# The adaLN modulation of a hybrid trunk: streaming its matrix past silu(c) in the kernel's opening

## The chip, the cores and the metric

The kernel runs on one core of one Trainium2 chip. The metric is the device time of one execution in microseconds; of several runs the median is given. The trace is of one profiled execution, with times from the start of its span.

## The reference, cut to what matters

One layer of a diffusion backbone (DEPTH is 1, so only the RG-LRU mixer and the SwiGLU run), on 2048 latent tokens and 256 context tokens of width 1024, all in float32:

```python
act_lat, act_ctx = silu(c), silu(c_ctx)
mx = split(act_lat @ mod_w + mod_b, 6)        # shift, scale, gate of both sub-layers
mc = split(act_ctx @ mod_w + mod_b, 6)
hx = rms_norm(x, g_mix) * (1 + mx[1]) + mx[0]
hc = rms_norm(ctx, g_mix) * (1 + mc[1]) + mc[0]
x = x + mx[2] * rglru_mixer(hc, hx)
x = x + mx[5] * swiglu(rms_norm(x, g_ffn) * (1 + mx[4]) + mx[3])
```

The opening needs the first two of the six parts, shift and scale, for the latents and for the context: two vectors of 1024 times a 1024 x 2048 matrix of 8 MB. The other four are needed much later, for the latents alone.

## The kernel before

The kernel works on transposed activations: 128 channels on the partitions, tokens along the free axis. `D` = 1024 channels are `KD` = 8 tiles; `C` = 512 tokens are one half of a super-tile of `S` = 1024. Large products run as three fp32r products each (`mm3`, lines 106 to 108: high x high, high x low, low x high); `parts` (lines 83 and 84) makes such a pair of an operand, a cast on ScalarE and the remainder on VectorE.

`sweep1` runs the RG-LRU over two super-tiles; `sweep2` does the output product, the second norm and the feed-forward. The change is in `begin`, the opening of `sweep1`. There the order on TensorE, ScalarE and VectorE is the order of the program text (`manual_schedule`); only the DMA queue of SyncE is ordered by a planner. A buffer of a tag is handed on when its last user is done. The tags that matter: `raw` (4 buffers of 1024 columns), `op` (6), `hx` (8), and `p2`, four PSUM pairs, one for each product in flight.

What `begin` does, in order:

1. Constants; silu of c and c_ctx (`self.sc`, 128 x 8 x 2) on ScalarE; `silu_row` spreads silu(c) over the partitions with two products of a diagonal (lines 138 and 142) and copies it (L212). `decay` computes the recurrence's constants on VectorE, with one Exp on ScalarE.
2. The modulation in four quarters q of 512 outputs (0 and 1: shift and scale of the first four channel tiles; 2 and 3: of the last four). `mod_load` fetches a quarter as two halves of 1 MB into `op` buffers. `mod_half` (L228) makes each 128 x 128 piece of the matrix the stationary operand and multiplies the two silu columns with it, so the result comes out with channels on the partitions. `mod_apply` adds the bias and makes `A` (scale) and `B` (shift).
3. `column_stats` (L284, L287, L288) sums squares of the context and of the first 512 latents over channel tiles: a square on ScalarE, a sum on VectorE. Small products (L602) finish the sums, `rstd_of` (L123 to L130) takes the inverse root in sixteen small VectorE steps, and `spread` with `bc_sbuf` (L148) makes rows of it that are equal on all partitions.
4. `apply`, for one channel tile: VectorE scales (L305), ScalarE adds the shift and casts (L306, the high part), VectorE takes the remainder (L307). Tiles 0 to 3 of the first half run while TensorE is in quarters 2 and 3; tiles 4 to 7 follow `mod_apply` of these, each with one `token_stats` (L275, squares of 128 tokens of the second half).
5. The first half of the first rec product (`project`, 8 tiles x 3 products of 512 columns), of the gate product, then the spread row of the second half (L340, L341), the context (`apply_context`, four pairs of tiles, the row's spread standing behind the first), its rec product, `apply` of the second half, and the second halves of rec and gate. Behind it `blocks` runs the other nineteen channel blocks.

The turn between the super-tiles (L740, L750, L751) already mixes `apply` of two tiles: the scale of tile k + 4 stands behind the remainder of tile k.

## Time and profile before

| | us |
|---|---|
| median of 3 runs | 2342.04 |
| lowest, highest | 2341.98, 2343.08 |
| the profiled execution | 2343.92 |
| its span | 2342.2 |
| TensorE busy | 2253.5 (96%) |
| VectorE busy | 1489.7 (64%) |
| ScalarE busy | 1156.4 (49%) |
| mean granted TensorE clock | 0.975 |

Engines are PE (TensorE's products), PEld (its weight loads, which overlap), DVE (VectorE), ACT (ScalarE), POOL and SP (the DMA queue). A busy PE is not a PE at its peak: products overlap and their ends are modelled, so the distance from one start to the next tells more than the length.

### The profile page before, as it was taken

The page shows a single profiled execution, that of the slowest core. Times are in us where ns is not written, and L with a number is a line of the kernel's source. Part 1 is how long each engine was busy: PE and PEld are TensorE (multiplying, and loading weights), DVE is VectorE, ACT ScalarE, POOL GpSimd, SP SyncE. Part 2 cuts the span into 40 slices and gives each one's busy share as a digit, 9 for nine tenths or more (in the row PEclk, how much of TensorE's full clock was granted, in tenths as well). Part 3 has the DMA queues.
Part 4 walks back from the last instruction along what each step waited for, and adds up shares of the span by engine and source line. Part 5 has one row for each costly group of instructions (what it writes and reads, how often), then busy time and mean ns, then how long its engine had stood idle before and what let it go on. Part 6 is the DMA issues. An engine that isn't in the chain of part 4 may idle for free.

```text
span 2342.2 us, 25844 instructions
## 1 busy us (share of the span) xinstructions
PE 2253.5 (96%) x9852; PEld 1852.4 (79%) x9852; DVE 1489.7 (64%) x1912; ACT 1156.4 (49%) x1399; POOL 0.7 (0%) x6
## 2 busy tenths in 40 slices
PE   8899999899999958999999999999999999999999
PEld 8578887688887846878787888778888888888887
DVE  4567888678887577676666546864555555545443
ACT  2357775687776335565646334443333333333332
POOL 0000000000000000000000000000000000000000
PEclk9799999999999978999999999999999999999999
DMA  7135555221114733434343666776422222236664
GB/s 280 41 140 207 204 178 207 85 73 63 63 63 154 250 127 112 150 127 164 126 163 121 204 227 225 242 263 232 162 81 81 81 81 81 87 129 224 227 215 143
DMA packets 126556, 356.23 MB, mean 152 GB/s; under 512 B 15072, under 2 KB 15072, under 8 KB 125408
## 3 DMA queue, kind: packets, MB, share of 16 engines
q1 hardware_dynamic: 126432, 354.58, 44.5%
q8 instruction: 77, 1.26, 0.2%
q14 instruction: 47, 0.39, 0.0%
HBM read 283.22 MB, written 71.30 MB: 151 GB/s over the span
## 4 chain that ended last, share of the span: by engine, by line
PE 68%; ACT 7%; DVE 3%; issue 2%; DMA 1%; SPq 0%; DVEq 0%; ACTq 0%
PE ps_dn L107 6%; PE ps_dn L108 6%; PE ps_dn L106 6%; PE ps_be L106 6%; PE ps_be L107 6%; PE ps_be L108 6%; PE ps_ep L108 3%; PE ps_ep L107 3%; PE ps_ep L106 3%; PE ps_wo L106 3%; PE ps_wo L107 3%; PE ps_wo L108 3%; ACT L77 2%; PE ps_rec L108 2%; PE ps_rec L107 2%
## 5 line engine op out<-in xcount | busy, mean ns | idle before, releaser
L107 PE MATMUL ps_dn<-op_xd,op_wd 128*128 128x512 f32 x704 | 275.2, 391 | 1.9 <-DVE op_xd L84 1.8
L108 PE MATMUL ps_dn<-op_xd,op_wd 128*128 128x512 f32 x704 | 274.7, 390 | 0.0
L106 PE MATMUL ps_dn<-op_xd,op_wd 128*128 128x512 f32 x704 | 270.4, 391 | 1.6 <-ACT op_xd L83 1.6
L84 DVE TENSOR_TENSOR op_wd<-raw_wd,op_wd 128x1024 fp32r<-128x1024 f32 x88 | 107.7, 1223 | 200.2 <-ACT op_wd L83 200.1
L83 ACT CAST op_wd<-raw_wd 128x1024 fp32r<-128x1024 f32 x88 | 92.7, 1053 | 270.1 <-PE ps_dn L108 221.1
L950 DVE TENSOR_TENSOR s<-ps_ep,s 128x512 f32<-128x512 f32 x88 | 60.6, 688 | 154.1 <-ACT s L975 104.9
L107 PEld LDWEIGHTS ps_dn<-op_xd,op_wd 128*128 128x128 f32 x704 | 132.6, 188 | 30.8 <-DVE op_xd L84 3.2
L106 PEld LDWEIGHTS ps_dn<-op_xd,op_wd 128*128 128x128 f32 x704 | 132.1, 188 | 30.2 <-ACT op_xd L83 2.4
L108 PEld LDWEIGHTS ps_dn<-op_xd,op_wd 128*128 128x128 f32 x704 | 132.7, 189 | 27.6
L106 PE MATMUL ps_be<-T,op_b 128*128 128x512 f32 x352 | 139.5, 396 | 9.5 <-ACT s L975 9.5
L77 ACT ACT_TABLE_LOAD x113 | 145.0, 1283 | 2.7 <-PEq L1109 0.7
L106 PE MATMUL ps_ep<-T,op_s 128*128 128x512 f32 x352 | 138.3, 394 | 8.3 <-ACT T L890 8.3
L108 PE MATMUL ps_be<-T,op_b 128*128 128x512 f32 x352 | 138.4, 393 | 0.0
L107 PE MATMUL ps_be<-T,op_b 128*128 128x512 f32 x352 | 138.2, 393 | 0.0
L387 DVE SCALAR_TENSOR_TENSOR u<-ps_rec,c_conv_w,u 128x1024 f32<-128x1024 f32 x60 | 77.1, 1285 | 95.2 <-ACT u L384 93.6
L107 PE MATMUL ps_ep<-T,op_s 128*128 128x512 f32 x352 | 137.4, 390 | 0.0
L108 PE MATMUL ps_ep<-T,op_s 128*128 128x512 f32 x352 | 137.4, 390 | 0.0
L108 PE MATMUL ps_gate<-hx,op_g 128*128 128x512 f32 x320 | 127.0, 397 | 5.5 <-DVE op_g L84 5.5
L106 PE MATMUL ps_rec<-hx,op_r 128*128 128x512 f32 x320 | 129.6, 405 | 2.1 <-ACT hx L306 2.1
L107 PE MATMUL ps_rec<-hx,op_r 128*128 128x512 f32 x320 | 129.4, 404 | 0.6 <-DVE hx L307 0.6
L975 ACT COPY s<-ps_be 128x512 f32<-128x512 f32 x44 | 25.6, 583 | 207.8 <-PE ps_be L108 207.8
L108 PE MATMUL ps_rec<-hx,op_r 128*128 128x512 f32 x320 | 127.7, 399 | 0.0
(256 smaller groups left out, 5380.4 us busy)
## 6 DMA issues: line engine op xcount, KB each, us to landing
raw_wd<-in_down SPq DMA_DIRECT2D x88, 512.0 KB, 3.6
raw_xd<-d_act SPq DMA_DIRECT2D x88, 512.0 KB, 4.6
raw_ga<-in_gu SPq DMA_DIRECT2D x44, 512.0 KB, 3.9
raw_gb<-in_gu SPq DMA_DIRECT2D x44, 512.0 KB, 4.3
d_act<-s SPq DMA_DIRECT2D x88, 256.0 KB, 3.5
raw_xo<-d_rg SPq DMA_DIRECT2D x40, 512.0 KB, 4.2
raw_mod<-in_mod_t SPq DMA_DIRECT2D x32, 512.0 KB, 5.4
x<-in_x_t SPq DMA_DIRECT2D x48, 256.0 KB, 5.7
```

Source lines behind the costliest of these rows:

```text
L77: return self.table(self.nc.scalar.activation(out, in_, func, bias=bias, scale=scale))
L83: nc.scalar.copy(t[:, 0, :], raw)
L84: nc.vector.tensor_tensor(out=t[:, 1, :], in0=raw, in1=t[:, 0, :].bitcast(F32), op=ALU.subtract)
L106: ins = mm(ps, w[0], x[0], start=first, stop=False, skip_group_check=shared)
L107: mm(ps, w[0], x[1], start=False, stop=False, skip_group_check=shared)
L108: mm(ps, w[1], x[0], start=False, stop=last, skip_group_check=shared)
L387: v.scalar_tensor_tensor(out=part, in0=ps, scalar=cw[:, i : i + 1], in1=part, op0=ALU.mult, op1=ALU.add)
L950: v.tensor_tensor(out=t, in0=ps, in1=t, op=ALU.add)
L975: nc.scalar.copy(s3, be)
```

## The change

Six parts. (1) `mod_quarter` takes the place of `mod_half` and `mod_bank`: the silu columns become the stationary operand, four columns wide, and the matrix streams past, 512 columns at a time. Of its eight k the first four run in plain float32 (`mod_z`: the two silu columns and two zero columns); the other four are split into high and low parts by `parts`, against `mod_st`, whose four columns are the high parts of silu and the remainders. The result is four rows; ScalarE copies them to a `raw` tile and small products with `sel` turn them back into columns, adding high and low rows. (2) The quarters are loaded into `hx` buffers, where the tiles made of the input go later. (3) The first rec weight is loaded into a `raw` buffer at the start, and all four quarters before the second x halves. (4) `apply` takes a list and puts the scale of the next tile behind the cast of this one. (5) The order in `begin`: quarter 0, context sums, quarter 1, `decay`, latent sums, the weight's split, quarter 2, rows, tiles 0 to 3, quarter 3, the four `token_stats` together, tiles 4 to 7. (6) `apply_context` takes all eight context tiles in one list, behind the gate product and the spread row.

```diff
--- before.py
+++ after.py
...
             row = self.spread(self.sc[:, 4 * q : 4 * q + 4, 0], f"silu{q}")
             self.nc.vector.tensor_copy(self.sc_row[:, q * C : (q + 1) * C], row)
+    def mod_operands(self):
+        nc = self.nc
+        z = self.cp.tile([P, KD, 4], F32, name="mod_z")
+        nc.vector.memset(z, 0.0)
+        nc.vector.tensor_copy(z[:, :, 0:2], self.sc)
+        st = self.cp.tile([P, KD, 4], F32R, name="mod_st")
+        nc.vector.tensor_copy(st, z)
+        nc.vector.tensor_tensor(out=st[:, :, 2:4], in0=self.sc, in1=st[:, :, 0:2].bitcast(F32), op=ALU.subtract)
+        sel = self.cp.tile([P, 2], F32, name="sel")
+        nc.vector.tensor_tensor(out=sel, in0=self.ident[:, 0:2], in1=self.ident[:, 2:4], op=ALU.add)
+        self.mod_z, self.mod_st, self.sel = z, st, sel
     def mod_load(self, q):
         ts = []
         for half in range(2):
-            t = self.wp.tile([P, KD // 2, C], F32, tag="op", name=f"modf{q}_{half}", bufs=OPS)
+            t = self.hp.tile([P, KD // 2, C], F32, tag="hx", name=f"modf{q}_{half}", bufs=KD)
             self.nc.sync.dma_start(t, self.io["mod_f"][q, half])
             ts.append(t)
         return ts
-    def mod_half(self, ps, t, half):
-        for kk in range(KD // 2):
-            k = half * (KD // 2) + kk
-            for i in range(4):
-                self.nc.tensor.matmul(ps[:, i, :], t[:, kk, i * P : (i + 1) * P], self.sc[:, k, :],
-                                      start=(k == i == 0), stop=(k == KD - 1 and i == 3), skip_group_check=True)
-    def mod_bank(self, q):
-        return self.bank(f"ps_mod{q}")[:, :8].rearrange("p (i s) -> p i s", s=2)
+    def mod_split(self, ts, q):
+        return [self.parts(ts[1][:, 2 * j : 2 * j + 2, :].rearrange("p a c -> p (a c)"), f"modf{q}_{j}")
+                for j in range(2)]
+    def mod_quarter(self, q, ts, hl):
+        nc = self.nc
+        ps = self.bank(f"ps_mod{q}")[:4]
+        for k in range(4):
+            nc.tensor.matmul(ps, self.mod_z[:, k, :], ts[0][:, k, :], start=(k == 0), stop=False)
+        for k in range(4, KD):
+            for w in range(2):
+                x = hl[(k - 4) // 2][:, w, (k % 2) * C : (k % 2 + 1) * C]
+                nc.tensor.matmul(ps, self.mod_st[:, k, :], x, start=False, stop=(k == KD - 1 and w == 1))
+        rows = self.wp.tile([P, S], F32, tag="raw", name=f"mod_rows{q}", bufs=RAWS)[:4, :C]
+        nc.scalar.copy(rows, ps)
+        pc = self.bank(f"ps_modc{q}")[:, :8].rearrange("p (i s) -> p i s", s=2)
+        for i in range(4):
+            nc.tensor.matmul(pc[:, i, :], rows[:, i * P : (i + 1) * P], self.sel[:4],
+                             start=(i == 0), stop=(i == 3), skip_group_check=True)
+        return pc
     def mod_apply(self, q, pc):
...
             v.tensor_tensor(out=x, in0=x, in1=wide(self.A), op=ALU.mult)
             v.tensor_tensor(out=x, in0=x, in1=wide(self.B), op=ALU.add)
-    def apply(self, x, bc, a, b, h, l):
+    def apply(self, items):
         v = self.nc.vector
-        v.scalar_tensor_tensor(out=x, in0=x, scalar=a, in1=bc, op0=ALU.mult, op1=ALU.mult)
-        self.nc.scalar.activation(h, x, AF.Identity, bias=b, scale=1.0)
-        v.scalar_tensor_tensor(out=l, in0=x, scalar=b, in1=h.bitcast(F32), op0=ALU.add, op1=ALU.subtract)
-    def apply_context(self, j, xc, bc):
-        nc = self.nc
-        t = self.hp.tile([P, 2, 2, TX], F32R, tag="hc", name=f"hc{j}", bufs=4)
-        for i in range(2):
-            k = 2 * j + i
-            self.apply(xc[:, k % 4, :TC], bc, self.A[:, k, 1:2], self.B[:, k, 1:2], t[:, i, 0, :TC], t[:, i, 1, :TC])
-        x = xc[:, 2 * j % 4 : 2 * j % 4 + 2, TC:]
-        nc.scalar.copy(t[:, :, 0, TC:], x)
-        nc.vector.tensor_tensor(out=t[:, :, 1, TC:], in0=x, in1=t[:, :, 0, TC:].bitcast(F32), op=ALU.subtract)
-        self.hc += [(t[:, i, 0, :], t[:, i, 1, :]) for i in range(2)]
+        def scale(x, bc, a, b, h, l):
+            v.scalar_tensor_tensor(out=x, in0=x, scalar=a, in1=bc, op0=ALU.mult, op1=ALU.mult)
+        scale(*items[0])
+        for i, (x, bc, a, b, h, l) in enumerate(items):
+            self.nc.scalar.activation(h, x, AF.Identity, bias=b, scale=1.0)
+            if i + 1 < len(items):
+                scale(*items[i + 1])
+            v.scalar_tensor_tensor(out=l, in0=x, scalar=b, in1=h.bitcast(F32), op0=ALU.add, op1=ALU.subtract)
+    def apply_context(self, xc, bc):
+        nc = self.nc
+        ts = [self.hp.tile([P, 2, 2, TX], F32R, tag="hc", name=f"hc{j}", bufs=4) for j in range(KD // 2)]
+        self.context_extra(xc, bc[:, 3 * P - 2 : 3 * P])
+        for j, t in enumerate(ts):
+            nc.scalar.copy(t[:, :, 0, TC:], xc[j // 2][:, 2 * j % 4 : 2 * j % 4 + 2, TC:])
+        self.apply([(xc[k // 4][:, k % 4, :TC], bc[:, :TC], self.A[:, k, 1:2], self.B[:, k, 1:2],
+                     ts[k // 2][:, k % 2, 0, :TC], ts[k // 2][:, k % 2, 1, :TC]) for k in range(KD)])
+        for j, t in enumerate(ts):
+            x = xc[j // 2][:, 2 * j % 4 : 2 * j % 4 + 2, TC:]
+            nc.vector.tensor_tensor(out=t[:, :, 1, TC:], in0=x, in1=t[:, :, 0, TC:].bitcast(F32), op=ALU.subtract)
+        self.hc = [(ts[k // 2][:, k % 2, 0, :], ts[k // 2][:, k % 2, 1, :]) for k in range(KD)]
     def hx_tiles(self, s):
         ts = [self.hp.tile([P, 2, S], F32R, tag="hx", name=f"hx{s}_{k}", bufs=KD) for k in range(KD)]
...
         self.A = self.cp.tile([P, KD, 2], F32, name="A_mix")
         self.B = self.cp.tile([P, KD, 2], F32, name="B_mix")
+        raw_r = self.raw(io["w_rec"][0], "r0")
+        mod[2] = self.mod_load(2)
+        mod[3] = self.mod_load(3)
+        self.constants_rest()
+        a, b = (lambda k: self.A[:, k, 0:1]), (lambda k: self.B[:, k, 0:1])
+        first, second = slice(0, C), slice(C, S)
+        self.mod_operands()
         self.silu_row()
+        pm, hl = {}, {}
+        hl[0] = self.mod_split(mod[0], 0)
+        pm[0] = self.mod_quarter(0, mod[0], hl[0])
+        acc = [self.column_stats([xc[k // 4][:, k % 4, :] for k in range(KD)], TX, "c")]
+        hl[1] = self.mod_split(mod[1], 1)
+        pm[1] = self.mod_quarter(1, mod[1], hl[1])
         self.decay()
-        pm = {q: self.mod_bank(q) for q in range(2)}
-        for q in range(2):
-            for half in range(2):
-                self.mod_half(pm[q], mod[q][half], half)
-        mod[2] = self.mod_load(2)
-        acc = [self.column_stats([xc[k // 4][:, k % 4, :] for k in range(KD)], TX, "c"),
-               self.column_stats([x0[k][:, :C] for k in range(KD)], C, "x")]
-        mod[3] = self.mod_load(3)
         for q in range(2):
             self.mod_apply(q, pm[q])
+        acc.append(self.column_stats([x0[k][:, :C] for k in range(KD)], C, "x"))
         ss = self.bank("ss_a")[:, :7]
-        for i, (a, t0) in enumerate([(0, 0), (0, P), (0, TX - P)] + [(1, j * P) for j in range(4)]):
-            nc.tensor.matmul(ss[:, i : i + 1], acc[a][:, t0 : t0 + P], self.ones[:, :1],
+        for i, (s, t0) in enumerate([(0, 0), (0, P), (0, TX - P)] + [(1, j * P) for j in range(4)]):
+            nc.tensor.matmul(ss[:, i : i + 1], acc[s][:, t0 : t0 + P], self.ones[:, :1],
                              start=(i == 0), stop=(i == 6), skip_group_check=True)
         y = self.rstd_of(ss, "rstd_a")
-        pm = {q: self.mod_bank(q) for q in (2, 3)}
-        self.mod_half(pm[2], mod[2][0], 0)
-        bc0 = self.bc_sbuf(self.spread(y[:, 3:], "n1_0"), "n1_0")
+        W["r", 0] = self.parts(raw_r, "r0")
+        hl[2] = self.mod_split(mod[2], 2)
+        diag = self.row_diag(y[:, 3:], "n1_0")
+        pm[2] = self.mod_quarter(2, mod[2], hl[2])
+        bc0 = self.row_bc(diag, "n1_0")
         bcc = self.bc_sbuf(self.spread(y[:, :3], "n1_c"), "n1_c")
-        self.mod_half(pm[2], mod[2][1], 1)
-        for half in range(2):
-            self.mod_half(pm[3], mod[3][half], half)
-        self.fetch(W, "r", blocks, 0)
-        self.constants_rest()
         hx = self.hx[0] = self.hx_tiles(0)
-        a, b = (lambda k: self.A[:, k, 0:1]), (lambda k: self.B[:, k, 0:1])
-        first, second = slice(0, C), slice(C, S)
-        for k in range(KD):
-            if k == KD // 2:
-                for q in (2, 3):
-                    self.mod_apply(q, pm[q])
-            self.apply(x0[k][:, first], bc0, a(k), b(k), hx[k][0][:, first], hx[k][1][:, first])
-            if k >= KD // 2:
-                y = self.token_stats(C, k - KD // 2, 4, "b")
+        item = lambda k, cols, bc: (x0[k][:, cols], bc, a(k), b(k), hx[k][0][:, cols], hx[k][1][:, cols])
+        self.apply([item(k, first, bc0) for k in range(4)])
+        hl[3] = self.mod_split(mod[3], 3)
+        pm[3] = self.mod_quarter(3, mod[3], hl[3])
+        for q in (2, 3):
+            self.mod_apply(q, pm[q])
+        for k in range(4):
+            y = self.token_stats(C, k, 4, "b")
+        self.apply([item(k, first, bc0) for k in range(4, KD)])
         for k in range(KD):
             nc.sync.dma_start(x0[k][:, second], io["x_t"][0][:, k, second])
         self.fetch(W, "g", blocks, 0)
-        wr, wg = W.pop(("r", 0)), W.pop(("g", 0))
+        t = W.pop(("r", 0))
+        wr, wg = (t[:, 0, :], t[:, 1, :]), W.pop(("g", 0))
         pr, pg = self.pair("ps_rec0_0"), self.pair("ps_gate0_0")
         self.project(0, pr, wr, (0,))
         diag = self.row_diag(y, "n1_1")
-        self.hc = []
-        self.context_extra(xc, bcc[:, 3 * P - 2 : 3 * P])
-        for j in range(KD // 2):
-            self.apply_context(j, xc[j // 2], bcc[:, :TC])
-            if j == 0:
-                self.project(0, pg, wg, (0,))
-                bc1 = self.row_bc(diag, "n1_1")
+        self.project(0, pg, wg, (0,))
+        bc1 = self.row_bc(diag, "n1_1")
+        self.apply_context(xc, bcc)
         psc = self.pair("ps_recc_0")[:, :TX]
         self.project(0, psc, wr, ctx=self.hc)
-        for k in range(KD):
-            self.apply(x0[k][:, second], bc1, a(k), b(k), hx[k][0][:, second], hx[k][1][:, second])
+        self.apply([item(k, second, bc1) for k in range(KD)])
         self.project(0, pr, wr, (1,))
         self.project(0, pg, wg, (1,))
         self.fetch(W, "r", blocks, 1)
```

## Rows read from the trace of the kernel before

**Rows 1.** Busy us by stage: sum, PE, PEld, DVE, ACT, POOL, clock, DMA share
```profile
0.00:70.70 70.70, 64.72 (x278) 59.94 (x279) 26.44 (x78) 15.95 (x27) 0.70 (x6) 1.00 0.62 232
...
93.00:103.50 10.50, 6.39 (x25) 4.68 (x23) 5.83 (x16) 4.48 (x11) 0.00 (x0) 0.64 0.17 51
...
103.50:120.30 16.80, 15.43 (x24) 6.30 (x25) 11.09 (x16) 6.45 (x9) 0.00 (x0) 0.50 0.00 0
...
127.40:341.20 213.80, 209.80 (x1035) 177.80 (x1034) 167.15 (x243) 148.35 (x191) 0.00 (x0) 0.99 0.52 183
```

**Rows 2.** Timeline of PE, first two quarters: start, length, engine, line
```profile
9.27 27.31 PE L228 MATMUL ps_mod<-silu_c,modf 128*128 128x2 f32 x128
```

**Rows 3.** Timeline of DVE, scales of two second-half tiles
```profile
104.11 0.74 DVE L305 SCALAR_TENSOR_TENSOR x<-x,A_mix,bcn 128x512 f32<-128x512 f32 x1
...
106.31 0.74 DVE L305 SCALAR_TENSOR_TENSOR x<-x,A_mix,bcn 128x512 f32<-128x512 f32 x1
```

**Rows 4.** Timeline of PE, products of the first rec unit
```profile
71.31 0.63 PE L107 MATMUL ps_rec<-hx,op_r 128*128 128x512 f32 x1
...
71.74 0.63 PE L108 MATMUL ps_rec<-hx,op_r 128*128 128x512 f32 x1
...
76.03 0.39 PE L107 MATMUL ps_rec<-hx,op_r 128*128 128x512 f32 x1
...
76.26 0.40 PE L108 MATMUL ps_rec<-hx,op_r 128*128 128x512 f32 x1
```

**Rows 5.** Groups up to 130 us by shape: busy, mean ns, idle before
```profile
L142 PE MATMUL silu_bc<-silu_diag,ones 128*128 128x512 f32 x4 | 4.2, 1141 | 5.3 <-DVE silu_diag L138 5.3
...
L83 ACT CAST op_r<-raw_r 128x1024 fp32r<-128x1024 f32 x3 | 3.1, 1042 | 0.0
...
L84 DVE TENSOR_TENSOR op_r<-raw_r,op_r 128x1024 fp32r<-128x1024 f32 x2 | 2.5, 1225 | 3.4 <-ACT op_r L83 3.4
...
L287 ACT ACTIVATE sq_x<-x 128x512 f32<-128x512 f32 x7 | 4.4, 630 | 0.8 <-DVE acc_x L288 0.7
...
L288 DVE TENSOR_TENSOR acc_x<-acc_x,sq_x 128x512 f32<-128x512 f32 x7 | 4.8, 692 | 1.1 <-ACT sq_x L287 0.4
...
L275 ACT ACTIVATE xtokb<-xtokb 128x1024 f32<-128x1024 f32 x4 | 4.2, 1043 | 0.0
...
L148 ACT COPY bcn<-n_bc 128x512 f32<-128x512 f32 x1 | 0.6, 586 | 23.9 <-PE n_bc L142 23.9
...
L305 DVE SCALAR_TENSOR_TENSOR xc<-xc,A_mix,bcn_c 128x256 f32<-128x256 f32 x8 | 3.8, 479 | 0.0
```

**Rows 6.** Timeline of ACT, table load before the first Sigmoid
```profile
149.82 1.28 ACT L77 ACT_TABLE_LOAD   x1
```

**Rows 7.** Timeline, the decay from Exp to its last instruction
```profile
10.61 0.22 ACT L77 ACTIVATE sp_e<-sp_e 128x20 f32<-128x20 f32 x1 [6.75 <-DVE sp_e L191]
...
15.76 0.17 DVE L206 TENSOR_SCALAR c_t<-sp_p 128x20 f32<-128x20 f32 x1
```

**Rows 8.** Timeline of DVE, first rstd and what follows
```profile
39.60 0.17 DVE L123 TENSOR_SCALAR rstd_a_m<-ss_a 128x7 f32<-128x7 f32 x1 [2.62 <-PE ss_a L602]
...
42.62 0.69 DVE L138 TENSOR_TENSOR n_diag<-ident,rstd_a_y 128x512 f32<-128x512 f32 x1
```

**Rows 9.** Timeline of DVE in the turn
```profile
411.09 1.28 DVE L740 SCALAR_TENSOR_TENSOR xr<-xr,A_mix,bcn 128x1024 f32<-128x1024 f32 x1
...
412.28 1.28 DVE L751 SCALAR_TENSOR_TENSOR hx<-xr,B_mix,hx 128x1024 fp32r<-128x1024 f32 x1
```

**Rows 10.** DMA issues up to 130 us: KB each, us to landing
```profile
raw_r<-in_w_rec SPq DMA_DIRECT2D x3, 512.0 KB, 3.5
```

**Rows 11.** Timeline of PE, end of first-half rec, third gate product
```profile
80.62 0.40 PE L108 MATMUL ps_rec<-hx,op_r 128*128 128x512 f32 x1
...
84.67 0.80 PE L108 MATMUL ps_gate<-hx,op_g 128*128 128x512 f32 x1 [2.47 <-DVE op_g L84]
```

**Rows 12.** Busy us from 20 to 30, columns as in rows 1, GB/s last
```profile
20.00:30.00 10.00, 10.00 (x48) 10.00 (x49) 4.80 (x8) 3.67 (x6) 0.00 (x0) 1.00 1.02 385
```

## The prediction, made before the changed kernel was run

> **What bounds the kernel now.** I read the busy times by stage first [rows 1]. In the long stretch behind the opening TensorE is busy 209.8 of 213.8 us: what the opening gains or loses by 127.4 us, where its last gate product ends, I carry to the end one for one. Inside the opening the bound changes. Up to 70.7 us TensorE is busy 64.7 us, mostly with small modulation products, VectorE 26.4. Two quarters of the matrix take 27.31 us, 13.65 each: every 128x128 piece is loaded to multiply two columns [rows 2]. Later VectorE and ScalarE set the end: scale, cast and remainder of one tile run strictly in turn, 2.20 us from one scale to the next [rows 3]. From 103.5 to 120.3 TensorE works at that pace, 15.4 us "busy" at a granted clock of 0.50.
>
> The clock must be read with care. The column says 1.00 up to 70.7, yet behind that the first wide products start 0.43 apart and later ones 0.23 apart [rows 4]. [...] So pure weight loads, without a pause, had not brought the upper level; wide products did.
>
> **The change, part by part.** Positions are microseconds of the new run, an estimate at each step.
>
> *Operands.* Five small VectorE instructions for the stationary operands stand in front of silu's row, 0.95 us. The row's second product ends at 10.4.
>
> *One quarter.* The matrix now streams, 512 columns an instruction, past four silu columns. [...] I take 1.86 at the lower level and half, 0.93, at the upper. Four k are split: eight products of 0.43 or 0.23. All lower is 7.4 + 3.4 = 10.9 us, all upper 3.7 + 1.8 = 5.6, against 13.65. No row shows a wide product with four stationary columns, so its level is the unknown that matters. I take half of the plain products at the lower price and the rest at the upper, 7.4 us, because wide products did raise the clock [rows 4] and these stream the same width. The loads of four columns I cost at nothing: a 512-wide product covers each. Uncovered, they would cost at most what loads cost now, 0.21 each (64 a quarter) [rows 2], 3.4 us for 16.
>
> *What it adds around a quarter.* ScalarE copies the rows out, 0.59, and eight small products turn them into columns, 1.0 to 1.7 (0.21 each at the lower level). Two casts of 1.04 on ScalarE and two remainders of 1.22 on VectorE split the second half [rows 5]. The copy is a new wait of ScalarE for TensorE: behind it, in order, stand the context's squares, the next casts and Exp, and VectorE's sums and the decay wait for those.
>
> *The chain.* Quarter 0 ends at 17.8, its copy at 18.4. The context's squares go at the pace of VectorE's sums, to 22.9. Quarter 1's remainders end at 25.8, its last products at 26.6, the copy at 27.2. Then Exp's table: in the kernel before nothing stood between Silu and Exp, so the load lay early; elsewhere it stands straight in front of its function, 1.28 us [rows 6]. So 28.5; Exp 28.7, decay polynomial 5.1 [rows 7], mod_apply 0.6: 34.4. [...]
>
> *Latent squares.* The raw tag has four buffers. The first weight block now takes one at the start and keeps it until its split behind rstd; two accumulators hold two. One is left, so a square (0.63) and its sum (0.69) run in turn [rows 5]: 8.7 us for seven, the first square being ready, to 43.1. With two buffers, as now, sums alone would take 4.8. TensorE hid this before; nothing hides it now. Sums over partitions 2.0, rstd 3.2 (fifteen steps of 0.20) [rows 8]: 48.3.
>
> *Quarters 2 and 3.* Three remainders (weight block, two of quarter 2) 3.7, last products 0.8, copy and columns 1.6, spread and its copy 1.8: 56.2. Four tiles, the scale of one beside the cast of another: where the turn already does this, VectorE's instructions start 1.19 us apart at 1.28 busy, without a gap [rows 9]. At half that width I take 0.70 each, 1.46 a tile with the handover: 62.5. Quarter 3's remainders 2.8, products 1.5: 66.8. The four token squares now stand ahead of the last four tiles instead of among them, 1.04 [rows 5] and a read-out, 1.25 each; the last one's tile waits for the row tile's buffer and a load of 3.5 us [rows 10]: 73.8. Rstd 3.4, four tiles 5.6: 82.8. The first rec product ends at 83.4; it ended at 81.0 [rows 11]. So the streamed matrix by itself, with what it adds, loses 2.4 us.
>
> *Behind it.* The gate product no longer stands 2.47 us for its weight's remainder [rows 11] and goes at the upper level: 89.4; the spread row 91.0, where the context's stage began at 93.0. Its eight tiles run unbroken, two VectorE instructions of 0.48 each [rows 5]: 99.2, products to 103.8, about as before. The eight second-half tiles take 8 x 1.4 = 11.3 us instead of 8 x 2.2 = 17.6: 110.5. Rec ends at 111.1, the gate, all at the upper level, at 116.4.
>
> *Loads.* The weight block and quarters 2 and 3 move ahead of the second x halves on SP's queue; modulation tiles use the hx buffers, so none waits for an op buffer. Ten megabytes end with quarter 2: at 385 GB/s [rows 12] from 5 us on, 31. Its casts come at 43. Cost nothing, covered by twelve microseconds of squares; without that cover, the delay itself. POOL's queue gets nothing.
>
> **Sum:** 127.4 to 116.4, 11.0 us. The profiled execution took 2343.92 (span 2342.2, 1.7 around it), 1.9 above the median of the runs, 2342.04. Taken off the median: 2331.0. Bounds: all quarters lower, 3.5 more each and 1.0 for small products, +15.0; all upper, about -4; two square buffers, -3.9; table load hidden, -1.3.
>
> **The rivals.** *The lower level stays* through all quarters. Against it: [rows 4]. For it: TensorE never paused up to 70 us and yet stayed lower, so not every kind of work raises it, and work in four of 128 stationary columns may be such a kind. Price +15.0, on the path because the copy holds ScalarE behind each quarter: the opening ends at 131.4, 4.0 later than now, 2346.0; with plain products near 2.28, up to 2349. It decides from 10.2 us a quarter on, where 2.75 more times four has eaten the 11.0. [...]
>
> *Token tiles come late.* All four loads, not the last alone, queue for raw buffers until quarter 3's row tile is free at 69.2. Then the squares start 3.5 us behind that and rstd ends 4 later: 2335. For it: the diagonal and two row tiles stand ahead in program order. Against: buffers come free behind rstd, 20 us earlier.
>
> *The edit does not do what it says:* the tiles don't overlap, 0.75 lost on each of sixteen, 12 us: 2343. Against it is the turn [rows 9]; little chance.
>
> **How the numbers follow.** Forecast 0.60, lower level 0.25, late tokens 0.12, no overlap 0.03. About 0.2%, 4.7 us, is what a measurement of this kernel can tell from no change. The forecast's own range is 2324 to 2337: one of the bounds of 4 with half of another below, half a quarter's doubt above. Faster: 0.59 of the forecast and 0.07 of late tokens, 0.66. The lower level lies at the edge of 2346.7: 0.13 slower and 0.12 same; with what is left of the others 0.20 same and 0.14 slower. The range, 2324 to 2346.5, leaves out the upper half of the lower-level case and a little below.
>
> **What would show it.** Products of quarters 1 to 3 starting 0.23 apart and quarters near 7 us; a square and a sum of the latents strictly in turn; a table load between the second row copy and Exp; the first rec product ending near 83 (98 at the lower level); second-half scales 1.4 apart; no wait in the first gate product; the last gate product ending near 116. It is wrong if the quarters' products stay 0.43 apart, if scales stay 2.2 apart, or if the time behind the opening changes too.

## The result and the profile after

| | before | after |
|---|---|---|
| median, us | 2342.01 | 2328.54 |
| lowest, highest | 2341.79, 2343.08 | 2327.99, 2329.23 |
| profiled execution, its span | 2343.92, 2342.2 | 2328.31, 2326.5 |
| mean granted TensorE clock | 0.975 | 0.977 |
| last gate product of the opening starts the next unit at | 127.39 | 111.56 |
| span behind that | 2214.8 | 2214.9 |

The ratio of the times is 0.9942, with a 95% interval of 0.9925 to 0.9959: faster, by 13.5 us of the medians and 15.6 of the two profiled executions. The last two rows of the table say where it came from: all of it lies in the opening, which is 15.8 us shorter. These are the two products, of the kernel before and of the changed one:

```profile
127.39 0.39 PE L106 MATMUL ps_rec<-hx,op_r 128*128 128x512 f32 x1
111.56 0.39 PE L106 MATMUL ps_rec<-hx,op_r 128*128 128x512 f32 x1
```

The lead over the kernel before grows step by step: 0.9 us at the end of the first rec product (81.0 and 80.1), 6.2 at the end of the gate product (91.9 and 85.7), 7.8 at the context's last tile (101.9 and 94.1), 14.2 at the last of the second-half tiles (119.6 and 105.4), 15.8 at the opening's end. So the gate product and the second-half tiles make most of it.

Busy times of the changed kernel by stage (columns: stretch and length, busy time and count of TensorE, its loads, VectorE, ScalarE and GpSimd, granted clock, DMA share, GB/s):

```profile
core 0: us, PE busy (x) PEld busy (x) DVE busy (x) ACT busy (x) POOL busy (x), PEclk, DMA share, GB/s
0.00:65.00 65.00, 40.79 (x119) 14.11 (x119) 35.88 (x91) 27.38 (x42) 0.70 (x6) 0.83 0.63 244
98.50:106.00 7.50, 6.52 (x26) 4.22 (x25) 7.18 (x12) 4.97 (x7) 0.00 (x0) 1.00 0.01 2
106.00:111.60 5.60, 5.60 (x26) 4.57 (x26) 5.25 (x9) 1.67 (x3) 0.00 (x0) 1.00 0.27 95
111.60:325.40 213.80, 209.78 (x1035) 177.80 (x1034) 168.62 (x246) 148.61 (x191) 0.00 (x0) 0.99 0.52 183
```

Against [rows 1]: the stage up to the first rec product, in which TensorE was busy nearly all the time, is 5.8 us shorter (the product starts at 64.98, not at 70.74) and two thirds busy; the second-half tiles' stage, which ran at a granted clock of 0.50, runs at 1.00; the long stretch behind is busy for the same 209.8 of 213.8 us.

TensorE's timeline through the four quarters (start, length, line, tiles, shape, count, and in brackets the idle time before and what ended it; L247 are the plain products, L251 the split ones, L256 the columns, L644 the sums over the partitions):

```profile
10.32 4.50 PE L247 MATMUL ps_mod<-modf,mod_z 128*4 128x512 f32 x8
14.76 2.01 PE L251 MATMUL ps_mod<-op_modf,mod_st 128*4 128x512 f32 x8
18.40 3.60 PE L247 MATMUL ps_mod<-modf,mod_z 128*4 128x512 f32 x8
23.75 1.99 PE L251 MATMUL ps_mod<-op_modf,mod_st 128*4 128x512 f32 x7 [0.86 <-DVE op_modf L84]
27.38 0.83 PE L644 MATMUL ss_a<-ones,acc_c 128*128 128x1 f32 x6
38.73 1.86 PE L644 MATMUL ss_a<-ones,acc_x 128*128 128x1 f32 x8 [10.52 <-DVE acc_x L314]
40.53 6.46 PE L247 MATMUL ps_mod<-modf,mod_z 128*4 128x512 f32 x8
46.91 2.01 PE L251 MATMUL ps_mod<-op_modf,mod_st 128*4 128x512 f32 x8
52.27 3.60 PE L247 MATMUL ps_mod<-modf,mod_z 128*4 128x512 f32 x8
58.37 0.39 PE L251 MATMUL ps_mod<-op_modf,mod_st 128*4 128x512 f32 x1 [2.51 <-ACT op_modf L83]
59.63 2.90 PE L251 MATMUL ps_mod<-op_modf,mod_st 128*4 128x512 f32 x7 [0.87 <-DVE op_modf L84]
```

And the granted clock of the same kernel around quarters 2 and 3:

```profile
30.00:46.00 16.00, 7.27 (x15) 2.64 (x16) 12.46 (x43) 5.97 (x8) 0.00 (x0) 0.50 0.59 219
46.00:48.00 2.00, 2.00 (x7) 0.43 (x6) 2.00 (x3) 0.00 (x0) 0.00 (x0) 0.92 0.63 238
48.00:58.00 10.00, 7.20 (x25) 2.42 (x22) 5.50 (x9) 5.08 (x8) 0.00 (x0) 1.00 0.33 107
60.00:66.00 6.00, 5.34 (x18) 3.06 (x15) 1.11 (x4) 3.44 (x6) 0.00 (x0) 0.50 0.00 0
```

Where 13.65 us of loads and two-column products stood [rows 2], a quarter is now 3.6 us of plain and 2.0 us of split products at the upper level, that of the products 0.23 apart in [rows 4]: plain instructions start 0.43 apart there, split ones 0.23. Quarter 2 pays 6.46 for the same plain products: TensorE had stood 10.52 us up to 38.73, the clock was at 0.50 when they began, and the first six started 0.85 apart. From 46 to 48 it reads 0.92 and behind that 1.00, while nothing but products with four stationary columns ran from 40.53 to 48.92. Quarter 3's split products stand 2.51 and 0.87 us for their casts and remainders, and behind that the clock falls back to 0.50.

ScalarE and VectorE of the changed kernel, at the places on which the opening turns (L314 sums of squares, L301 token squares, L333, L337 and L340 scale, cast and remainder, L376 the spread row's copy):

```profile
26.37 1.28 ACT L77 ACT_TABLE_LOAD   x1
27.66 0.22 ACT L77 ACTIVATE sp_e<-sp_e 128x20 f32<-128x20 f32 x1
33.22 5.46 DVE L314 TENSOR_TENSOR acc_x<-acc_x,sq_x 128x512 f32<-128x512 f32 x7
68.75 1.06 ACT L301 ACTIVATE xtokb<-xtokb 128x1024 f32<-128x1024 f32 x1 [2.49 <-DMA xtokb<-in_x]
69.93 0.17 DVE L123 TENSOR_SCALAR rstd_b_m<-ss_b 128x4 f32<-128x4 f32 x1 [4.48 <-ACT xtokb L301]
72.80 1.41 DVE L333 SCALAR_TENSOR_TENSOR x<-x,A_mix,bcn 128x512 f32<-128x512 f32 x2
86.80 0.58 ACT L376 COPY bcn<-n_bc 128x512 f32<-128x512 f32 x1 [8.03 <-PE n_bc L375]
88.20 0.48 DVE L340 SCALAR_TENSOR_TENSOR hc<-xc,B_mix,hc 128x256 fp32r<-128x256 f32 x1 [5.81 <-ACT hc L337]
96.52 0.75 DVE L333 SCALAR_TENSOR_TENSOR x<-x,A_mix,bcn 128x512 f32<-128x512 f32 x1
97.85 0.75 DVE L333 SCALAR_TENSOR_TENSOR x<-x,A_mix,bcn 128x512 f32<-128x512 f32 x1
```

The second-half scales are 1.33 apart, where they were 2.20 [rows 3]. Three waits of this order show. The decay's steps on VectorE, between Exp and 33.1, hold back the latents' sums. The fourth token tile holds the rstd, and with it tiles 4 to 7, for 4.48 us. And the context's casts stand on ScalarE behind the copy of a spread row that the context does not need, until 88.20.

### The profile page after: what moved, and what is told of

It reads as the page before. It is cut to its first block, busy times and chain, and to the rows that moved or that the text cites. A ratio compares the mean times of both kernels' runs of the same rounds, so it can differ in the third digit from the quotient of the medians.

```text
span 2326.5 us, 25556 instructions
## 1 busy us (share of the span) xinstructions
PE 2212.5 (95%) x9692; PEld 1801.2 (77%) x9692; DVE 1497.0 (64%) x1925; ACT 1166.0 (50%) x1411; POOL 0.7 (0%) x6
## 4 chain that ended last, share of the span: by engine, by line
PE 69%; ACT 7%; DVE 4%; issue 2%; DMA 1%; DVEq 0%; ACTq 0%
PE ps_dn L107 6%; PE ps_dn L108 6%; PE ps_dn L106 6%; PE ps_be L106 6%; PE ps_be L107 6%; PE ps_be L108 6%; PE ps_wo L106 3%; PE ps_wo L107 3%; PE ps_wo L108 3%; PE ps_ep L108 3%; PE ps_ep L107 3%; PE ps_ep L106 3%; ACT L77 2%; PE ps_rec L106 2%; PE ps_rec L107 2%
## 5 line engine op out<-in xcount | busy, mean ns | idle before, releaser
L108 PEld LDWEIGHTS ps_dn<-op_xd,op_wd 128*128 128x128 f32 x704 | 132.7, 189 | 27.7
L106 PE MATMUL ps_rec<-hx,op_r 128*128 128x512 f32 x320 | 127.4, 398 | 3.9 <-ACT hx L337 3.9
L106 PE MATMUL ps_wo<-op_xo,op_wo 128*128 128x512 f32 x320 | 124.0, 393 | 5.7 <-ACT r L77 5.7
L107 PE MATMUL ps_rec<-hx,op_r 128*128 128x512 f32 x320 | 127.7, 399 | 1.0 <-DVE hx L340 1.0
```

The costliest lines, as they stand in the source:

```text
L106: ins = mm(ps, w[0], x[0], start=first, stop=False, skip_group_check=shared)
L107: mm(ps, w[0], x[1], start=False, stop=False, skip_group_check=shared)
L108: mm(ps, w[1], x[0], start=False, stop=last, skip_group_check=shared)
```

## The experiments

All are edits of the changed kernel but the second, which edits the kernel before. The opening's end is the start of the first product behind its last gate product. The span behind it is 2211.7 to 2216.3 us in all these runs, without a pattern, so the opening's end tells more of an edit than the time does. It is read from one profiled execution of each, in which the clock need not fall and rise at the same places. Each ratio is against the kernel before, on the same chip.

| edit | median, us | ratio, 95% interval | opening ends |
|---|---|---|---|
| none (the change) | 2328.54 | 0.9942, 0.9925 to 0.9959 | 111.56 |
| tiles strictly in turn | 2347.54 | 1.0019, 1.0009 to 1.0029 | 132.30 |
| kernel before, second-half tiles overlapped | 2332.85 | 0.9965, 0.9952 to 0.9978 | 118.56 |
| matrix stationary again | 2328.07 | 0.9949, 0.9933 to 0.9965 | 114.41 |
| context's sums late | 2331.63 | 0.9955, 0.9940 to 0.9970 | 114.63 |
| context ahead of the row's copy | 2322.19 | 0.9915, 0.9901 to 0.9930 | 106.67 |
| two token squares later | 2320.66 | 0.9905, 0.9891 to 0.9920 | 102.38 |
| quarters 1 and 3 plain | 2324.77 | 0.9923, 0.9909 to 0.9938 | 106.24 |
| decay early | 2319.78 | 0.9900, 0.9884 to 0.9917 | 108.27 |
| context's extra remainders first | 2328.89 | 0.9940, 0.9925 to 0.9954 | 111.75 |
| three edits together | 2314.09 | 0.9878, 0.9861 to 0.9894 | 97.93 |
| the three and decay early | 2307.06 | 0.9845, 0.9831 to 0.9860 | 91.83 |

**Which part carries the gain: the overlap.** First the changed kernel with `apply` in turn:

```diff
-        scale(*items[0])
         for i, (x, bc, a, b, h, l) in enumerate(items):
+            scale(x, bc, a, b, h, l)
             self.nc.scalar.activation(h, x, AF.Identity, bias=b, scale=1.0)
-            if i + 1 < len(items):
-                scale(*items[i + 1])
```

> The changed kernel with scale, cast and remainder of each tile strictly in turn again. Theory (the gain is made where two tiles overlap on VectorE and ScalarE): 3.0 us more for tiles 0 to 3, 3.0 for tiles 4 to 7, 5.4 for the eight context tiles and 6.6 for the second half, so the last gate product of the opening ends 18 us later than the changed kernel's 111.6, near 129.6; time near 2346, no better than before. Rival (the streamed matrix carries the gain): at most 6 us more, near 2334.

VectorE's timeline of it, second-half tiles:

```profile
105.94 0.75 DVE L333 SCALAR_TENSOR_TENSOR x<-x,A_mix,bcn 128x512 f32<-128x512 f32 x1
107.47 0.75 DVE L338 SCALAR_TENSOR_TENSOR hx<-x,B_mix,hx 128x512 fp32r<-128x512 f32 x1 [0.79 <-ACT hx L337]
108.14 0.75 DVE L333 SCALAR_TENSOR_TENSOR x<-x,A_mix,bcn 128x512 f32<-128x512 f32 x1
```

The pace is 2.20 again and the opening ends 20.7 us later, 2.1 of it in the last gate product, which goes partly at the lower level (7.6 us instead of 5.5). Without the overlap the change is slower than the kernel before. The other way round, the kernel before with only its eight second-half tiles overlapped:

```diff
-            self.apply(x0[k][:, second], bc1, a(k), b(k), hx[k][0][:, second], hx[k][1][:, second])
...
+            nc.scalar.activation(hx[k][0][:, second], x0[k][:, second], AF.Identity, bias=b(k), scale=1.0)
+            if k + 1 < KD:
+                nc.vector.scalar_tensor_tensor(out=x0[k + 1][:, second], in0=x0[k + 1][:, second], scalar=a(k + 1),
+                                               in1=bc1, op0=ALU.mult, op1=ALU.mult)
```

> The kernel before, with nothing changed but the eight second-half tiles, where the scale of the next tile stands behind the cast of this one. Theory: tiles 1.4 us apart and not 2.2, so the opening ends 6.6 us earlier, near 120.8, and the time is near 2335.4. Rival (TensorE, at its lower level here, then sets the pace, or the gate product behind gives it back): within 2 us of 2342.

VectorE's timeline of it:

```profile
104.88 0.75 DVE L647 SCALAR_TENSOR_TENSOR x<-x,A_mix,bcn 128x512 f32<-128x512 f32 x1
106.21 0.75 DVE L647 SCALAR_TENSOR_TENSOR x<-x,A_mix,bcn 128x512 f32<-128x512 f32 x1
```

The scales are 1.33 apart and the opening ends at 118.56 instead of 127.39, 8.8 us earlier. Of this 6.6 are the tiles themselves (11.1 us instead of 17.7), as expected; some 1.7 more come behind them, mostly because the gate product now goes at the upper level throughout (5.5 us instead of 6.7), and 0.6 lie ahead of the edit and are not its own. That is the largest single part of the gain, got without streaming anything. The other large step, the first gate product, needs neither the overlap nor the streaming: it takes 5.7 us in the change, 6.4 with the tiles in turn and 6.0 with the matrix stationary (the next run), against 10.9 before, each counted from the end of the rec product. It came with the new order, in which the weight's remainder no longer stands behind the rstd of the tokens; no run takes that part away alone.

**What the streamed matrix is worth.** The changed kernel with the matrix as the stationary operand again, no casts, rows or columns:

```diff
-        for k in range(4):
-            nc.tensor.matmul(ps, self.mod_z[:, k, :], ts[0][:, k, :], start=(k == 0), stop=False)
...
+        for k in range(KD):
+            for i in range(4):
+                nc.tensor.matmul(pc[:, i, :], ts[k // 4][:, k % 4, i * P : (i + 1) * P], self.sc[:, k, :],
+                                 start=(k == i == 0), stop=(k == KD - 1 and i == 3), skip_group_check=True)
```

> The changed kernel with the matrix stationary again (128x128 pieces times two columns, no casts, no rows to copy, no columns to rebuild), everything else as changed. Theory: quarters of 13.65 us; the first ends at 24, the second at 38, and the latents' sums behind mod_apply then end at 44; third at 59.5, fourth at 77; first rec product ends near 87.5 instead of 80.1, time near 2336: streaming is worth 7 us in this order. Rival (streaming gives nothing by itself, as predicted: its own additions eat it): first rec product near 80 to 82, time near 2329.

The rival came nearer: the first rec product ends at 82.61 (80 to 82 said, 87.5 by the theory) and the opening 2.85 us later than with the streamed matrix; the times cannot be told apart. TensorE's timeline and its stretches show why:

```profile
45.59 13.79 PE L247 MATMUL ps_mod<-silu_c,modf 128*128 128x2 f32 x64
62.22 10.69 PE L247 MATMUL ps_mod<-silu_c,modf 128*128 128x2 f32 x64
```

```profile
62.00:64.00 2.00, 2.00 (x18) 1.85 (x17) 1.82 (x3) 1.58 (x3) 0.00 (x0) 1.00 0.84 207
64.00:66.00 2.00, 2.00 (x18) 2.00 (x17) 2.00 (x4) 0.86 (x2) 0.00 (x0) 0.87 0.14 55
66.00:68.00 2.00, 2.00 (x11) 2.00 (x10) 1.79 (x4) 1.67 (x4) 0.00 (x0) 0.50 0.00 0
```

Quarter 3 costs 10.69 us here, for it began at the upper level (18 products in the first 2 us shown, 11 in the last), and it needs no cast, row or column. (What had raised the level is not shown: wide spread products stand just ahead, but in the kernel before the same products, 46.25 to 50.4, were followed by pieces 0.21 us apart.) By comparison, the streamed quarter 3 takes 12.8 from 52.27 to the last column at 65.05. The streamed form's lead can be followed as it goes. Quarter 1 is done at 27.46 instead of 37.43, 10.0 us earlier; the latents' sums, behind the decay, 5.1 earlier (38.7, 43.8); the copy of the spread row, with quarter 2, 9.6 (51.73, 61.34); the first rec product starts 7.8 earlier, for the long quarter 3, and ends 2.5 earlier: with the stationary matrix the four token squares are all done beside quarter 3, where no row tile holds a buffer for the last one to wait for.

**The mis-sized term, put back.** The prediction gave the latents' squares one buffer. In the trace the context's accumulator came free at 27.38, when its sums ran, and left two. Here it is kept:

```diff
-        for i, (s, t0) in enumerate([(0, 0), (0, P), (0, TX - P)] + [(1, j * P) for j in range(4)]):
+        cols = list(enumerate([(0, 0), (0, P), (0, TX - P)] + [(1, j * P) for j in range(4)]))
+        for i, (s, t0) in cols[3:] + cols[:3]:
```

> The changed kernel with the three small products that sum the context's squares over the partitions put behind the four of the latents, so that the context's accumulator keeps its raw buffer until the latents' squares are done. Theory (the latent squares took 5.5 us and not the 8.7 of the prediction because that buffer came free early and gave them a second square): a square and a sum go strictly in turn, 1.3 us apart, the sums end at 41.5 to 42.5 instead of 38.7, and the opening ends about 3 us later, near 114.5: about 2331.5. Rival (the squares were fast for another reason, such as the next square starting as soon as the sum has read its operand): the sums still go 0.80 apart and the opening ends at 111.6, 2328.5.

VectorE's timeline of it:

```profile
33.07 0.69 DVE L314 TENSOR_TENSOR acc_x<-acc_x,sq_x 128x512 f32<-128x512 f32 x1
34.45 0.69 DVE L314 TENSOR_TENSOR acc_x<-acc_x,sq_x 128x512 f32<-128x512 f32 x1 [0.69 <-ACT sq_x L313]
41.38 0.69 DVE L314 TENSOR_TENSOR acc_x<-acc_x,sq_x 128x512 f32<-128x512 f32 x1 [0.69 <-ACT sq_x L313]
```

A square and a sum go in turn, 1.38 apart; the seven take 9.0 us instead of 5.46. The sums end 3.4 us later than in the change, the first rec product 3.3 later, at 83.37, and the opening 3.1 later. That 83.37 meets the prediction's 83.4 so closely is in part luck: the three products moved behind the latents' add 1.4 us of their own (43.86 to 45.21), and the clock, which rose sooner, gave 1.7 back (quarter 2's plain products took 5.59 us instead of 6.46, the columns of quarter 3 1.05 instead of 1.86).

**The two waits on the way to the tiles.** The context ahead of the row's copy:

```diff
-        bc1 = self.row_bc(diag, "n1_1")
         self.apply_context(xc, bcc)
+        bc1 = self.row_bc(diag, "n1_1")
```

> The changed kernel with the spread row of the second half copied behind the context's tiles and not ahead of them. Theory (VectorE stands 5.8 us before the context's first remainder only because ScalarE's copy waits in order for TensorE's gate product): the context's tiles end near 88.5 instead of 94.0, second-half tiles start 5.5 us earlier, the opening ends near 106, time near 2323. Rival (TensorE is the bound there, or the context's product then waits for something else): within 1.5 us of 2328.5.

```profile
83.35 0.49 DVE L340 SCALAR_TENSOR_TENSOR hc<-xc,B_mix,hc 128x256 fp32r<-128x256 f32 x1 [0.18 <-ACT hc L337]
```

That first remainder of the context (VectorE's timeline) waits 0.18, not 5.81, and starts 4.85 us earlier; the opening ends 4.9 us earlier. Then two token squares and the rstd behind tiles 4 to 7:

```diff
-        for k in range(4):
-            y = self.token_stats(C, k, 4, "b")
+        for k in range(2):
+            self.token_stats(C, k, 4, "b")
         self.apply([item(k, first, bc0) for k in range(4, KD)])
...
+        for k in range(2, 4):
+            y = self.token_stats(C, k, 4, "b")
```

> The changed kernel with two of the four token squares, and the rstd behind them, moved behind the tiles 4 to 7 (which need neither). Theory (the tiles 4 to 7 start at 72.8 only because VectorE and ScalarE stand 4.5 us in the rstd's wait for the fourth token tile, and then in the rstd): the tiles start at about 65.5, the first rec product ends near 74 instead of 80.1, the context's stage begins 5 to 6 us earlier, the last gate product of the opening ends near 106 instead of 111.6: about 2323. Rival (the spread row, made later, is the next wait, or the gate product's weight comes late behind the squares): TensorE stands behind the first rec product, the gate ends where it does now, the opening ends at 110 to 112 and the time is 2327 to 2329.

```profile
64.07 1.41 DVE L333 SCALAR_TENSOR_TENSOR x<-x,A_mix,bcn 128x512 f32<-128x512 f32 x2
```

```profile
66.00:72.00 6.00, 5.15 (x19) 3.03 (x18) 5.00 (x7) 4.52 (x7) 0.00 (x0) 1.00 0.31 126
```

The first line is VectorE's, the second a stretch. The tiles start at 64.07 instead of 72.80 and the gate product at 70.58 instead of 80.09, more than was expected. TensorE no longer stands 3.95 us in the first rec product and works it at the upper level (clock 1.00); the rstd lies beside the gate product. The opening is 9.2 us shorter. Some 1.4 of it is not the edit's: quarter 3's columns, which stand ahead of it, ended at 63.63 instead of 65.05. The level took another course in this run. It was lost earlier, beside the spread products and the first plain products of quarter 3, and was back before the split ones:

```profile
52.00:54.00 2.00, 2.00 (x4) 0.22 (x3) 1.42 (x2) 1.31 (x3) 0.00 (x0) 0.50 0.88 258
```

The plain products took 4.40 us instead of 3.60, the clock at 0.85 from 54 to 56, but the wait for the cast was shorter (1.32 instead of 2.51), and the split products and the columns (1.98 and 1.05 us instead of 2.90 and 1.86) went at 1.00.

**Half in plain float32, or all.** Quarters 1 and 3 wholly plain:

```diff
-        for k in range(4):
-            nc.tensor.matmul(ps, self.mod_z[:, k, :], ts[0][:, k, :], start=(k == 0), stop=False)
-        for k in range(4, KD):
+        plain = q in self.plain
+        for k in range(KD if plain else 4):
+            nc.tensor.matmul(ps, self.mod_z[:, k, :], ts[k // 4][:, k % 4, :], start=(k == 0),
+                             stop=plain and k == KD - 1)
+        for k in () if plain else range(4, KD):
```

> The changed kernel with quarters 1 and 3 wholly in plain float32: no casts and remainders for them, eight k of two instructions each, 0.43 an instruction at the upper level. Theory (the split products of quarters 1 and 3 wait for casts that stand behind other work on ScalarE and VectorE, 0.9 us in quarter 1 and 3.4 in quarter 3): quarter 3 ends near 59.5 instead of 62.5, quarter 1 at 25.5 instead of 25.7, the opening's last gate product ends 2 to 4 us earlier than 111.6: about 2325. Rival (half-price split products are worth their casts, since eight plain k take twice 3.6 us and at the lower level twice that): quarter 3 ends at 62 or later and the opening ends at 111 to 114, 2328 to 2331.

TensorE's timeline of quarter 3, and one stretch:

```profile
51.54 7.03 PE L252 MATMUL ps_mod<-modf,mod_z 128*4 128x512 f32 x16
59.23 1.05 PE L262 MATMUL ps_modc<-sel,mod_rows 4*128 4x2 f32 x8 [0.67 <-ACT mod_rows L259]
```

```profile
58.00:60.00 2.00, 1.33 (x9) 0.77 (x7) 0.00 (x0) 1.40 (x2) 0.00 (x0) 1.00 0.00 0
```

Sixteen products in 7.03 us without a wait, at the upper level throughout; the columns take 1.05 instead of 1.86, at a clock of 1.00 where the change had 0.50. The opening ends 5.3 us earlier. In quarter 3 the split costs more than it saves: its products take about half the time (2.0 us for eight at the upper level, 3.6 for as many plain instructions), but they wait for casts that stand behind other work, and in the change the clock was at 0.50 behind these waits. Quarter 1's products end at 24.9 instead of 25.7, of which 0.5 is an earlier start.

**The decay's place.** Its constants between the split and the products of quarter 0:

```diff
         hl[0] = self.mod_split(mod[0], 0)
+        self.decay()
...
-        self.decay()
```

> The changed kernel with the decay's constants moved forward, from behind quarter 1 to behind the split of quarter 0, where VectorE waits for the rows of quarter 0 anyway. Theory (the table load and the sixteen-odd small VectorE steps between quarter 1 and the latents' sums, 27.7 to 33.1, lie on the path, as the prediction counted them, while TensorE stands and loses its clock): the latents' sums start near 28 instead of 33.2, quarter 2 near 35.5 instead of 40.5, and the opening's last gate product ends near 106.5 instead of 111.6: about 2323.5. Rival (the loads are the next wait: the latents' or quarter 2's second half land only as they are needed now): the sums or quarter 2's casts wait for DMA and the opening ends at 109 to 112, 2326 to 2329.

VectorE's timeline:

```profile
19.46 3.62 DVE L314 TENSOR_TENSOR acc_c<-acc_c,sq_c 128x258 f32<-128x258 f32 x7
29.73 0.17 DVE L269 TENSOR_TENSOR A_mix<-ps_modc,mod_b 128x8 f32<-128x8 f32 x1 [3.86 <-PE ps_modc L256]
31.76 4.67 DVE L314 TENSOR_TENSOR acc_x<-acc_x,sq_x 128x512 f32<-128x512 f32 x6 [0.63 <-ACT sq_x L313]
```

The latents' sums are done at 36.4 instead of 38.7 and the opening ends 3.3 us earlier, not 5: the decay pushed the context's sums and with them quarter 1, and behind waits of 1.32 and 0.86 us TensorE lost its level before quarter 1's columns (1.86 us for the eight):

```profile
26.00:28.00 2.00, 1.33 (x4) 0.30 (x3) 0.00 (x0) 0.80 (x2) 0.00 (x0) 0.51 1.01 418
```

The rival's loads were not the wait. The time fell by more than the opening did, 8.8 us between the medians; the profiled spans differ by 6.1, of which 2.8 lie behind the opening; what made them there stays open.

**A long wait that costs nothing.** The context's extra remainders ahead of its tiles (the block of L353 moved above the list of L333):

```diff
+        for j, t in enumerate(ts):
+            x = xc[j // 2][:, 2 * j % 4 : 2 * j % 4 + 2, TC:]
...
         self.apply([(xc[k // 4][:, k % 4, :TC], bc[:, :TC], self.A[:, k, 1:2], self.B[:, k, 1:2],
```

> The changed kernel with the remainders of the context's extra columns ahead of its eight tiles instead of behind them, so that the context's products need not wait for the last of the list. Theory (TensorE's wait of 5.63 us there is off the path: VectorE's chain of tiles sets the end of the second rec product): the products follow the tiles, TensorE's wait moves to the second-half tiles, and the opening ends where it did or up to 0.9 us later (the first scale now stands behind the extra casts): 111.6 to 112.5, 2328.5 to 2329.5. Rival (those products are on the path): the opening ends 3 to 4 us earlier, about 2325.

TensorE's timeline:

```profile
96.08 0.79 PE L106 MATMUL ps_rec<-hx,op_r 128*128 128x512 f32 x1 [0.92 <-ACT hx L337]
100.85 0.50 PE L107 MATMUL ps_rec<-hx,op_r 128*128 128x512 f32 x1 [0.36 <-DVE hx L340]
```

TensorE's wait of 5.63 us in the context's product is gone and the second rec product starts 2.5 us earlier, but then waits at every tile; the opening ends where it did.

**Together.** The context's, the token squares' and the plain quarters' edits in one kernel:

> Three edits together: the context's tiles ahead of the second-half spread row's copy, two token squares and the rstd behind the tiles 4 to 7, quarters 1 and 3 in plain float32. Theory (each takes away a wait of its own): the gains add up, 4.9 of the first as measured, 5 to 6 and 2 to 4 of the others, and the opening's last gate product ends at 97 to 99 instead of 111.6: 2314 to 2316. Rival (they shorten the same wait): the opening ends at 103 or later, 2319 or more.

And with the decay early as well:

> The three edits together (context's tiles ahead of the row's copy, two token squares behind the tiles 4 to 7, quarters 1 and 3 in plain float32) and the decay's constants moved forward as well. Theory: what the decay gives by itself comes on top of the 97.9 of the three, an opening that ends near 93, about 2309. Rival (with quarter 1 in plain float32 the time from quarter 1 to the latents' sums is already bound by TensorE or by loads): 96 to 98, 2312 to 2314.

The opening ends at 97.93 and 91.83, the times are 2314.09 and 2307.06 us: both beat both kernels, the second by 35.8 us under the kernel before it was run against. The first came out at its number for a partly wrong reason. Alone the three edits gave 4.9, 9.2 and 5.3, in sum 19.4, together 13.6. With the token squares moved, the context's first remainder waited only 1.38 us for its cast, so about 4.4 of the 5.81 were gone before the context's edit. The other 1.4 are those that were not the token squares' own: quarter 3's columns end at 60.28 with the plain quarters alone and at 60.45 with all three, so an earlier end of quarter 3 could be had only once. The decay gave 6.1 on top, more than its 3.3 alone. With quarter 1 plain it has no remainders of it to push back, and the latents' sums are done 5.3 us earlier (32.9 instead of 38.2), where the decay alone gave 2.3; the other 0.9 are quarter 2's plain products, in which the level rose sooner (5.53 us instead of 6.41).

## Why the prediction was right, step by step

The times of the main steps, predicted and in the profile after:

| step | predicted | measured |
|---|---|---|
| silu's row | 10.4 | 10.4 |
| quarter 0's products end | 17.8 | 16.8 |
| quarter 1's products end | 26.6 | 25.7 |
| Exp begins | 28.5 | 27.7 |
| latents' squares summed | 43.1 | 38.7 |
| quarter 2's products end | 52.8 | 48.9 |
| tiles 0 to 3 | 62.5 | 58.2 |
| rstd of the tokens | 77.2 | 72.8 |
| first rec product ends | 83.4 | 80.1 |
| gate product ends | 89.4 | 85.7 |
| context's tiles | 99.2 | 94.0 |
| second-half tiles | 110.5 | 105.4 |
| last gate product | 116.4 | 111.6 |

- *Direction and mechanism* were right: the gain comes from the second-half tiles and from gate products that no longer wait and go at the upper level, and the time behind the opening did not move. From 94.0 on the forecast's lengths hold: tiles 11.1 (11.3 said), gate 5.5 (5.3).
- *The time* came nearer than the mechanism: 2331.0 said and 2328.5 measured, 2.5 apart, while the opening's end is 4.8 apart. The prediction took its 11.0 us off the median before, 2342.04, but the profiled execution from which it read 127.4 had been 1.9 slower than that. That this hid two fifths of the miss is luck.
- *Latent squares* is the term that was mis-sized: 5.46 us, not 8.7. The prediction held that one raw buffer was left. The context's accumulator keeps its buffer only until its three sums have run, and TensorE was free for them at 27.38. With the buffer kept, the same seven take 9.0. The 3.2 us of this one term are as much as the whole difference up to the end of the first rec product (83.4 and 80.1), the smaller ones cancelling.
- *The context's tiles* run 0.79 apart, not 0.96, 1.4 to 1.6 us in all. Together with the squares that is the 4.8 us by which the opening ended earlier than predicted.
- *One quarter*: 7.4 was predicted. At the upper level it is 5.6; as they came, with their waits and levels, the four took 6.5, 7.3, 8.4 and 10.3. No run shows the 1.86 and 0.93 that were taken for a plain product with four stationary columns, at the lower and the upper level; its two instructions went 0.85 and 0.43 apart, 1.71 and 0.86 (in quarter 2 from 40.53, in quarters 1 and 3).
- *"So the streamed matrix by itself, with what it adds, loses 2.4 us"* was wrong as put. The first rec product ended 0.9 us earlier than before, and with the matrix stationary it ended 2.5 later. By the opening's end it gains, but only 2.85 us of 15.8, with the levels that the two executions happened to have; the times do not show it.
- *The table load* stood where it was put, 1.28 long, and Exp follows at once: 1.31 us from the end of the row copy (26.35) to Exp (27.66).
- *Rival, the lower level stays*: refuted for these products by quarters 0, 1 and 3 (2.01 us for the eight split ones of quarter 0, 3.60 for the eight plain instructions of the others), and by the rise at 46. It did return behind waits of TensorE (0.50 from 30 to 46 and from 60 to 66), but in quarter 2 the clock rose from 0.50 to 1.00 with only products with four stationary columns running.
- *Rival, token tiles late*: only the fourth was, as the forecast's own chain had it, but the price was larger than the load. Moving two squares and the rstd gave 9.2 us, 1.4 of them not the edit's: the tiles had stood behind the rstd's steps as well as behind the load.
- *Rival, no overlap*: refuted by the 1.33 between scales; its price was low, 12.0 said and 20.7 measured; the prediction counted sixteen tiles, but the eight of the context fall back into turn as well (4.8 us), and the last gate product loses part of the upper level (2.1).
- *The gate product without a wait*: so it was, 80.09 to 85.7.
- What the prediction did not see: the copy of the spread row stands ahead of the context's casts on ScalarE. It took the context's stage to begin behind that row, here 87.4, and did not ask whether it must: with the copy behind it, the context's first remainder ran at 83.35.

## What to carry to other kernels

When two engines work a list of tiles in turn, put the next tile's first step beside this tile's second: the second-half tiles alone gave 8 of the 15.8 us, with the products behind them, and it costs two lines. Then look at each instruction of an in-order engine for the wait that stands ahead of work which does not need it: three such moves and the plain quarters gave another 19.7 us here. Count a shared buffer's holders at the time of use, by what frees each, not by who takes one. A wait of the engine that bounds the whole kernel (5.63 us of TensorE) is worth nothing where another engine's chain ends later.

## What the runs showed of the hardware

- In the changed kernel the granted clock rose from 0.50 to 0.92 and 1.00 behind 46, with only products of 512 columns against four stationary columns running since 40.53. In the run with the stationary matrix it was not held by work on 128 stationary columns with two columns streamed: TensorE was busy all 6 us from 62 to 68, and the clock went 1.00, 0.87, 0.50, the count of products 18, 18, 11 in 2 us each.
- The recorded clock alone did not tell the level here; the pace had to be read beside it. In the same run it reads 1.00 from 54 to 58, with 11 products in each 2 us, and 1.00 from 62 to 64, with 18.
- A plain float32 product of 512 columns with four stationary columns took two instructions, 0.43 apart at the upper level, 0.86 (3.60 us for the eight instructions of four products, the last of them 0.59 long); a split one 0.23 (2.01 us for eight, the last 0.39 long).
- What followed a wait of TensorE cost time besides the wait: behind 2.51 and 0.87 us of standing in quarter 3 the clock fell to 0.50, and 60 to 66 went at that (columns 1.86 instead of 1.05 us, rec products 0.43 apart instead of 0.23). It stayed at 1.00 from 58 to 64 where the quarter was plain and TensorE stood no longer than 0.67 us up to 63.
- The length of the wait did not tell by itself whether the level was lost. Behind 1.32 and 0.87 us in quarter 3 of the run with the token squares moved it stayed at 1.00; behind 1.32 and 0.86 in quarter 1 of the run with the decay early it fell to 0.51 (26 to 28). In the former it had been at 0.50 from 52 to 54, though TensorE had not stood longer than 0.66 us since 41.
